# Where loads, PSUM banks and projection fill stand around the attention start of a hybrid decoder layer

## The chip, the cores and the metric

The kernel runs on one core of a Trainium2 chip. A core has five engines with queues of their own: PE (TensorE, matrix products), DVE (VectorE), ACT (ScalarE), POOL (GpSimd) and SP (SyncE, which here only issues DMAs). Transfers run on 16 DMA engines that all queues share. The metric is the device time of one execution in microseconds; lower is better.

## The reference

One layer of a decoder trunk on 1024 tokens of width 1024, with 16 learned meta tokens put in front. Everything is float32.

```python
u = rmsnorm(h, attn_norm_w[l])
proj = u @ w_in[l]
gq, gk, gv, gz, gb, ga, fq, fk, fv, ff = jnp.split(proj, IN_SPLITS, axis=-1)
o_gdn = gated_deltanet_group(jnp.concatenate([gq, gk, gv], axis=-1), gz, gb, ga, ...)
o_fox = forgetting_attention_group(fq, fk, fv, ff, fgate_b[l])
h = h + jnp.concatenate([o_gdn, o_fox], axis=-1) @ w_out[l]
h = h + swiglu(rmsnorm(h, ffn_norm_w[l]), w_gate[l], w_up[l], w_down[l])
h = rmsnorm(h, final_norm_w)
```

The first group (gated DeltaNet, 4 heads of 128) runs a delta rule over 64-token chunks: a triangular solve inside each chunk and a state carried from chunk to chunk. The second ("fox", 8 heads of 64) is causal softmax attention whose logits carry the difference of two cumulative log forget gates.

## The kernel before

Each float32 operand is split into a high part (a cast, on ACT, line 163) and a low part (the rest, on DVE, line 164); each product is three matmuls (`mm3g`, line 212): high by high, high by low, low by high. So weights that arrive by DMA (`load_w`, line 180, tiles raw_*) need two casts (whi_*, wlo_*) before PE can use them.

The program runs in stages: norms; DeltaNet projections and their convolution; the solve of the 64-token chunks, prepared by small 32-by-32 inverses (DVE steps on the tile up, lines 527 and 529); then the stage that the change touches; then attention; then the output projection of the fox half and the feed-forward network.

**Order of PE.** From the touched stage on, PE's order is written by a planner (`PeOrder`). It keeps a model time, chains with due times (generators that yield when their next step is ready), and one generator of fill. A chain step that is due runs first; otherwise the fill goes on by one matmul. The chains are `levels(0)` and `levels(1)` (the rest of the triangular solve, two heads each, due at model times that come from `LV0`), `scan()` (8 chunks of the state; po, os, on and then the transposes ot belong to it) and `csum` (the cumulative forget gate). The fill `fox()` is the projection work: z0 in 8 tiles, fv1 and fv0 (values, two column halves, one meta tile and 8 token tiles each), fk0 to fk3 and fq0 to fq3 (keys and queries, three column thirds each, named by their first column: 16, 358 and 700 for queries). What of the fill is left when the last chunk is out is run down before attention. In attention (`attention`, `scores`, `values`) the chain makes scores (sc), exponentials (pr, ACT line 1019), transposes (pt, line 1055) that ACT and DVE split into ph and pl (phm for the meta tokens), and value products (po, lines 1075, 1078 and 1079). Its fill is `wout_gdn`, the output projection of the DeltaNet half (tiles wog); DVE adds the input rows to it in ht (line 1175).

**Order of the rest.** On ACT, DVE, POOL and in SP's DMA queue the order is set by a scheduler that simulates a timeline of its own; `tc.issue_after(x)` makes it place an instruction behind x. Each queue runs in order. SP's DMAs share eight completion semaphores in turn, so each waits for the DMA eight places before it.

**Buffers.** A value tile of fv is split into fvt (3 buffers) and stored to v_d in DRAM (line 940). A key or query third is split into fhl (2 buffers, ACT line 768, DVE line 769) and stored to k_d or q_d (line 771). `att_head(h)` loads a head's keys, queries and values back (ka, qa, kk, sa, avt; lines 737 to 746) and, from head 1 on, the meta-token values: `vm_load` issues 8 loads of 8 KB per head (line 728), for heads 0 and 1 together behind head 1's loads. PSUM has one bank for general products (`ps_mm`, tag mm), two for po (tag pv, `ps_v`), two for scores, three for transposes. While `rot` is not zero, `ps_mm` turns over mm and both pv banks; at zero it gives the one mm bank.

Of the kernel before, what the change touches and what calls it, by code (L numbers as in the profile page):

```python
# [9 lines left out]
F32 = mybir.dt.float32  # L10
F32R = mybir.dt.float32r
# [4 lines left out]
P = 128  # L16
# [13 lines left out]
GQ, GK, GV, GZ, FQ, FK, FV = 0, 512, 1024, 1536, 2056, 2568, 3080  # L30
TCH = ((0, 348), (348, 346), (694, 346))
GRP = 4
LV0 = (76.0, 119.0)
LAT = 0.4
ATT0 = 3.0
LEAD = 0.6
# [61 lines left out]
def tile_hymba_layer(ctx, tc, x, meta, attn_norm_w, w_in, conv_w, a_log, dt_bias, gdn_norm_w,  # L98
                     fgate_b, w_out, ffn_norm_w, w_gate, w_up, w_down, final_norm_w, out):
    nc = tc.nc  # L100
# [11 lines left out]
    rot = [1]  # L112
# [11 lines left out]
    def ps_v(name):  # L124
        return bank("pv", 2, name)
# [469 lines left out]
    def levels(hp):  # L595
        na = lp.tile([P, 2, NT, P], F32, tag="na", bufs=2, name=f"na_{hp}")
        tb = lp.tile([P, 2, NT, 32], F32, tag="tb", bufs=2, name=f"tb_{hp}")
        ubk = lp.tile([P, 2, NT, 32], F32, tag="ubk", bufs=2, name=f"ubk_{hp}")
        nc.sync.dma_start(ubk, ud_d[hp].rearrange("b j h t k -> (b j) h t k"))
        for i in range(2):  # L600
            nc.sync.dma_start(na[:, i], rec_d[:, :, 0, 2 * hp + i].rearrange("t p c -> p t c"))
        if not hp:
            lv_t["act"], lv_t["dve"] = tail[0]
        with tc.issue_after(lv_t["dve"].ins):
# [96 lines left out]
        yield from mm3g(acc[:rows, :n], [(uh[:, k, col:col + rows], ul[:, k, col:col + rows], w[0][k][:, :n],  # L701
                                          w[1][k][:, :n]) for k in range(KT)], n / 2400)

    last = [None]

    fox_ws = [(GZ, 256, "z0"), (FV + 256, 264, "fv1"), (FV, 256, "fv0"), (FK, 256, "fk0"), (FK + 256, 256, "fk1"),
              (FQ, 256, "fq0"), (FQ + 256, 256, "fq1")]
# [1 line left out]

    def fox_load():  # L710
        if fox_ws:
            fox_w.append(win_block(*fox_ws.pop(0)))

    t_ld, hds, fixed, fq_m, h_ld = [], {}, [], [0], {}

# [203 lines left out]
    def fox():  # L919
        fox_load()  # L920
        w = fox_w.pop(0)
        for t in range(NT):
            if t == 1:
                fox_load()
            acc = ps_mm(f"z0_{t}")
            yield from proj_tmg(acc, t, w, 256)
            gate_out(t, acc, *((fvp, "fvt") if t < NT - 2 else (fp, "fhl")), 0)
        for b in (1, 0):
            n = 256 + 8 * b
            w = fox_w.pop(0)  # L930
            for t in range(-1, NT):
                if t == 1:
                    fox_load()
                col, rows = tok_cols(t)
                acc = (ps_mm if b or t % 2 else ps_t)(f"fv{b}_{t}")
                yield from proj_tmg(acc, t, w, n)
                vt = fvp.tile([P, 4, 2, DH], F32R, tag="fvt", name=f"fvt{b}_{t}")
                av = acc[:rows, :256].rearrange("p (h d) -> p h d", d=DH)
                split(vt[:rows, :, 0], vt[:rows, :, 1], av)
                nc.sync.dma_start(v_d[4 * b:4 * b + 4, col:col + rows].rearrange("h t d -> t h d"),  # L940
                                  vt[:rows].rearrange("p h a d -> p h (a d)").bitcast(F32))
                if b:
                    nc.vector.tensor_copy(fr[:rows, NT if t < 0 else t], acc[:rows, 256:264])
        fvc.close()
        yield from fox_proj(lambda m: k_d[m], TCH, 0, 1.0, "fk")
        od.add(csum(), od.t + 8.0)
        yield from fox_proj(lambda m: q_d[m].rearrange("a p c -> p a c"), ((NM, 342), (NM + 342, 342), (NM + 684, 340)), NM, -DH ** -0.5, "fq")

    lv_left, outs_left = {0, 1}, set(range(NT))
    for hp in range(2):  # L950
        od.add(levels(hp), LV0[hp] - 8.0)
    od.fill = fox()
    peo = ExitStack()
    peo.enter_context(tc.manual_schedule(engines={mybir.EngineType.PE}))
# [12 lines left out]
    od.add(scan(), od.t + 4.0, front=True)  # L967
    od.run(lambda: not outs_left)
    scc.close()
    while od.step_fill():  # L970
        pass
    uctx.close()

    alc = ExitStack()
    als.append(alc.enter_context(tc.tile_pool(name="alo", bufs=1)))
    atc = ExitStack()
    ap_ = atc.enter_context(tc.tile_pool(name="ap", bufs=1, side="right"))
    ap2 = atc.enter_context(tc.tile_pool(name="ap2", bufs=1, side="right"))
    rsum = ap_.tile([P, FH, NT], F32, name="rsum")
    for i in range(2):  # L980
        vms.append(ap2.tile([P, GRP, P], F32R, name=f"vm{i}"))
        nc.gpsimd.memset(vms[i].bitcast(F32), 0.0)
    att_tiles(1)
    masks = []

    def scores(h, g, hd, out):
# [54 lines left out]
    def values(h, g, hd, pts):  # L1041
# [1 line left out]
        nk = GRP * (g + 1)  # L1043
        nm = f"{g}_{h}"
        box = []
        for kt in (0, -1, *range(1, nk)):
            c0, j0 = NM + P * kt, max(0, kt - GRP * g)
            yield max(r for _, r in pts)
            pt = ps_t(f"pt_{nm}_{kt}")
# [18 lines left out]

            def av(kt=kt, ph=ph, pl=pl, q=q):
                if kt == 0:  # L1070
                    box.append(ps_v(f"po_{nm}"))
                po = box[0]
                if kt < 0:
                    for j in range(GRP):
                        nc.tensor.matmul(po[:, P * j:P * j + P], vms[h % 2][:, j], ph, start=False, stop=False)
                    od.pe(0.2135)
                    return
                nc.tensor.matmul(po[:, q], vt[:, kt], ph[:, q], start=kt == 0, stop=False)
                nc.tensor.matmul(po[:, q], vt[:, kt], pl[:, q], start=False, stop=(kt == nk - 1))
                od.pe((512 - q.start) / 1200)  # L1080
                if kt == nk - 1:
                    oa = ap2.tile([P, 512], F32, tag="oa", bufs=2, name=f"oa_{nm}")
                    nc.scalar.copy(oa, po)
                    od.on("act", 0.5)
                    for i in range(2):
                        last_o[0] = nc.gpsimd.dma_start(
                            o_d[GRP * g:GRP * g + GRP, rows, 4 * i + m].rearrange("t p c -> p t c"),
                            v3(oa[DH * i:DH * i + DH], GRP))
# [4 lines left out]
    def attention():  # L1093
# [3 lines left out]
        def score_stream():  # L1097
            for i, (h, g) in enumerate(groups):
                if h not in hds:
                    with tc.issue_after(last[0].ins) if h == 1 else nullcontext():  # L1100
                        hds[h] = att_head(h)
                ptl[i] = []
                for n, rdy in enumerate(scores(h, g, hds[h], ptl[i])):
                    pos[0] = i + n / (5, 9)[g]
# [10 lines left out]
                yield r  # L1115

        yield from ahead(1.0)
        rot[0] = 0
        for i, (h, g) in enumerate(groups):
            nt = GRP * (g + 1) + 1  # L1120
            yield from ahead(i + 1.0)
# [607 lines left out]
```

## Time and profile before

| what | value |
|---|---|
| median of three runs | 1305.55 us (1304.69 to 1306.87) |
| the profiled execution | 1305.29 us |
| its span, first to last instruction | 1303.6 us, mean granted TensorE clock 0.996 |
| PE busy | 1281.6 us, 98% of the span |
| DVE, ACT, POOL busy | 839.7, 547.7, 348.8 us |
| moved by DMA | 232.07 MB, mean 178 GB/s |

PE is the engine to watch: idle PE time is what a change of order can win or lose. The projection and scan stage lies between about 200 and 440 us, attention between 440 and 590, and the rest is the output projection and the feed-forward network. In rows of a timeline the bracket at the end gives the engine's idle time before the instruction, and what it waited for.

### The profile page before, as it was taken

Reading aid. Unit: us, or ns where it says so; the run is one execution under the profiler, and the core shown is the slowest. Engines: PE = TensorE matmul, PEld = TensorE weight load, DVE = VectorE, ACT = ScalarE, POOL = GpSimd, SP = SyncE. Lnnn points to the kernel's source line nnn. Section 1 sums busy time; section 2 is a strip of 40 time slices with the busy share of each in tenths; the row PEclk is TensorE's granted clock in tenths of the full one; section 3 lists DMA queues with packets and bytes.
Section 4 is the critical chain, followed back from the end, with each engine's and each line's share of the span. In section 5 each row is a group of like instructions: output and inputs, shape, how many; then the busy total and the mean of one; then the engine's idle time right before and its main releaser. Section 6 shows DMA issues by size and latency. Waiting matters only on the chain.

```text
span 1303.6 us, 20023 instructions
## 1 busy us (share of the span) xinstructions
PE 1281.6 (98%) x7434; PEld 1127.5 (86%) x7434; DVE 839.7 (64%) x1508; ACT 547.7 (42%) x940; POOL 348.8 (27%) x316
## 2 busy tenths in 40 slices
PE   9999999899999999999999999999999999999997
PEld 8999999899999888887778888888888888888886
DVE  6667898583246768886887666556666664365645
ACT  6455444142223557884553333233333343433332
POOL 2012213101022221112504534455334443020301
PEclk9999999999999999999999999999999999999999
DMA  6333625854389886737435644553444467945513
GB/s 230 99 118 110 183 86 141 234 143 154 127 285 304 220 236 190 183 94 253 168 114 161 198 165 155 186 163 129 159 155 166 165 212 268 393 178 197 207 64 129
DMA packets 185248, 232.07 MB, mean 178 GB/s; under 512 B 19816, under 2 KB 138176, under 8 KB 182336
## 3 DMA queue, kind: packets, MB, share of 16 engines
q1 hardware_dynamic: 182256, 222.15, 53.1%
q0 software_dynamic: 2896, 8.65, 2.2%
q8 instruction: 58, 0.95, 0.3%
q14 instruction: 38, 0.31, 0.1%
HBM read 153.11 MB, written 77.65 MB: 177 GB/s over the span
## 4 chain that ended last, share of the span: by engine, by line
PE 87%; DVE 5%; DMA 3%; issue 2%; SPq 1%; ACT 1%; POOL 0%; POOLq 0%; DVEq 0%; ACTq 0%
PE xp L1610 9%; PE yp L1610 7%; PE ua L1435 5%; PE ga L1435 5%; PE gb L1435 5%; PE ud L1435 5%; PE gd L1435 5%; PE ub L1435 5%; PE pj_fk L212 4%; PE pj_fq L212 3%; PE fv L212 3%; PE ue L1435 2%; PE ge L1435 2%; PE pt L1055 2%; PE wog L212 2%
## 5 line engine op out<-in xcount | busy, mean ns | idle before, releaser
L164 DVE TENSOR_TENSOR al_p<-ra_p,ah_p 128x2048 fp32r<-128x2048 f32 (+1 forms) x21 | 47.7, 2273 | 94.5 <-ACT ah_p L163 94.5
L163 ACT CAST ah_p<-ra_p 128x2048 fp32r<-128x2048 f32 (+1 forms) x21 | 37.1, 1767 | 106.2 <-PE xp L1610 47.9
L1610 PE MATMUL xp<-wl_p,ah_p 128*128 128x512 f32 (+1 forms) x176 | 67.3, 382 | 0.0
L1610 PE MATMUL xp<-wh_p,al_p 128*128 128x512 f32 (+1 forms) x176 | 67.3, 382 | 0.0
L1610 PE MATMUL xp<-wh_p,ah_p 128*128 128x512 f32 (+1 forms) x176 | 67.3, 382 | 0.0
L1491 POOL TENSOR_TENSOR gzw<-gzw,uzt 128x512 f32<-128x512 f32 x11 | 18.4, 1673 | 168.0 <-DVE uzt L1480 138.9
L1435 PE MATMUL gb<-uh_p,w_g_p 128*128 128x512 f32 x176 | 57.8, 389 | 0.0
L1435 PE MATMUL ub<-uh_p,w_u_p 128*128 128x512 f32 x176 | 57.7, 389 | 0.0
L1435 PE MATMUL gd<-uh_p,w_g_p 128*128 128x512 f32 x176 | 57.7, 389 | 0.0
L1435 PE MATMUL ud<-uh_p,w_u_p 128*128 128x512 f32 x176 | 57.7, 389 | 0.0
L163 ACT CAST ph<-pt 128x512 fp32r<-128x512 f32 (+1 forms) x96 | 45.2, 474 | 29.8 <-PE pt L1055 28.8
L164 DVE TENSOR_TENSOR pl<-pt,ph 128x512 fp32r<-128x512 f32 (+1 forms) x96 | 52.0, 554 | 8.4 <-ACT ph L163 7.8
L1491 POOL TENSOR_TENSOR gxy<-gxy,uxy 128x512 f32<-128x512 f32 x22 | 39.0, 1771 | 64.7 <-DVE uxy L1480 53.7
L164 DVE TENSOR_TENSOR w_u_p<-raw_u,w_u_p 128x512 fp32r<-128x512 f32 x42 | 41.9, 997 | 21.6 <-ACT w_u_p L163 21.5
L1019 ACT ACTIVATE pr<-pr,sm 128x144 f32<-128x144 f32 (+3 forms) x64 | 50.5, 791 | 10.0 <-DVE sm L1014 9.8
L1435 PE MATMUL ua<-uh_p,w_u_p 128*128 128x512 f32 x160 | 52.5, 389 | 0.0
L1435 PE MATMUL ga<-uh_p,w_g_p 128*128 128x512 f32 x160 | 52.5, 389 | 0.0
L1610 PE MATMUL yp<-wh_p,ah_p 128*128 128x512 f32 x132 | 51.3, 389 | 0.0
L1610 PE MATMUL yp<-wl_p,ah_p 128*128 128x512 f32 x132 | 51.3, 389 | 0.0
L1610 PE MATMUL yp<-wh_p,al_p 128*128 128x512 f32 x132 | 51.3, 389 | 0.0
L163 ACT CAST w_u_p<-raw_u 128x512 fp32r<-128x512 f32 x42 | 26.0, 620 | 55.7 <-PE gd L1435 36.0
L164 DVE TENSOR_TENSOR wl_p<-rw_p,wh_p 128x2048 fp32r<-128x2048 f32 (+1 forms) x21 | 46.5, 2212 | 3.8 <-ACT wh_p L163 3.8
(649 smaller groups left out, 4233.0 us busy)
## 6 DMA issues: line engine op xcount, KB each, us to landing
ra_p<-ao_p SPq DMA_DIRECT2D x14, 1024.0 KB
raw_g<-in_w_gate_dram SPq DMA_DIRECT2D x22, 512.0 KB
raw_u<-in_w_up_dram SPq DMA_DIRECT2D x22, 512.0 KB
raw_d<-in_w_down_dram SPq DMA_DIRECT2D x22, 512.0 KB
wt_p<-raw_d SPq DMA_DIRECT2D x33, 256.0 KB
rw_p<-wt_p SPq DMA_DIRECT2D x8, 1024.0 KB
rw_p<-in_w_down_dram SPq DMA_DIRECT2D x6, 1024.0 KB
ao_p<-gzw SPq DMA_DIRECT2D x22, 256.0 KB
```

The costliest lines, as they stand in the source:

```text
L163: cast = nc.scalar.copy(dst_hi, src)
L164: low = nc.vector.tensor_sub(dst_lo, src, dst_hi.bitcast(F32))
L212: nc.tensor.matmul(dst, a, b, start=first, stop=last)
L1019: nc.scalar.activation(pr[:, :n], pr[:, :n], AF.Exp, bias=sm[:, np_ - 1:np_], scale=-1.0, accum_out=rsum[:, h, j:j + 1])
L1055: nc.tensor.transpose(pt[:, P * j:P * j + P], pts[j][0][:, j, c0:c0 + P], ident)
L1435: nc.tensor.matmul(dst, a[:, c], b[:, k], start=(first and k == 0 and i == 0), stop=(k == 3 and i == 2), skip_group_check=not first)
L1491: last_mul[0] = G.tensor_tensor(gs[d], gs[d], us[d], op=ALU.mult)
L1610: nc.tensor.matmul(dst[:, n_], a[:, f, c], b[:, f, n_], start=(first and i == 0 and n == 0), stop=(i == NF - 1 and n == 2), skip_group_che ...
```

## The change

- `LV0` is smaller, and the levels' chains are added 20 instead of 8 below it: the solve, and with it the scan, enter PE's order sooner.
- The loads of the levels (ubk, na) are placed behind the last key or query store, or, where there is none yet, behind the last value store (`vst`). The projection weights' loads, while no key or query store exists, are placed behind the last value store.
- The tiles of attention that head 1 uses, the memsets of vm and head 1's loads are requested right after the scan's last chunk, ahead of the fill that is left; the clause that put head 1's loads behind the last query store is gone. As two heads' loads have then been requested when attention's fill starts, the loads of ht that SP issued go to POOL.
- In `values`, for the second half of the queries of a head (8 key tiles), the meta tile comes after the fourth key tile instead of after the first.
- `rot` becomes zero with the first po and not before the first value step, so attention's fill turns over three banks until then.

```diff
--- before.py
+++ after.py
@@ -30,7 +30,7 @@
 GQ, GK, GV, GZ, FQ, FK, FV = 0, 512, 1024, 1536, 2056, 2568, 3080
 TCH = ((0, 348), (348, 346), (694, 346))
 GRP = 4
-LV0 = (76.0, 119.0)
+LV0 = (72.0, 106.0)
 LAT = 0.4
 ATT0 = 3.0
 LEAD = 0.6
@@ -596,9 +596,10 @@
         na = lp.tile([P, 2, NT, P], F32, tag="na", bufs=2, name=f"na_{hp}")
         tb = lp.tile([P, 2, NT, 32], F32, tag="tb", bufs=2, name=f"tb_{hp}")
         ubk = lp.tile([P, 2, NT, 32], F32, tag="ubk", bufs=2, name=f"ubk_{hp}")
-        nc.sync.dma_start(ubk, ud_d[hp].rearrange("b j h t k -> (b j) h t k"))
-        for i in range(2):
-            nc.sync.dma_start(na[:, i], rec_d[:, :, 0, 2 * hp + i].rearrange("t p c -> p t c"))
+        with tc.issue_after((last[0] or vst[0]).ins):
+            nc.sync.dma_start(ubk, ud_d[hp].rearrange("b j h t k -> (b j) h t k"))
+            for i in range(2):
+                nc.sync.dma_start(na[:, i], rec_d[:, :, 0, 2 * hp + i].rearrange("t p c -> p t c"))
         if not hp:
             lv_t["act"], lv_t["dve"] = tail[0]
         with tc.issue_after(lv_t["dve"].ins):
@@ -701,7 +702,7 @@
         yield from mm3g(acc[:rows, :n], [(uh[:, k, col:col + rows], ul[:, k, col:col + rows], w[0][k][:, :n],
                                           w[1][k][:, :n]) for k in range(KT)], n / 2400)
 
-    last = [None]
+    last, vst = [None], [None]
 
     fox_ws = [(GZ, 256, "z0"), (FV + 256, 264, "fv1"), (FV, 256, "fv0"), (FK, 256, "fk0"), (FK + 256, 256, "fk1"),
               (FQ, 256, "fq0"), (FQ + 256, 256, "fq1")]
@@ -709,7 +710,8 @@
 
     def fox_load():
         if fox_ws:
-            fox_w.append(win_block(*fox_ws.pop(0)))
+            with tc.issue_after(vst[0].ins) if vst[0] and not last[0] else nullcontext():
+                fox_w.append(win_block(*fox_ws.pop(0)))
 
     t_ld, hds, fixed, fq_m, h_ld = [], {}, [], [0], {}
 
@@ -937,7 +939,7 @@
                 vt = fvp.tile([P, 4, 2, DH], F32R, tag="fvt", name=f"fvt{b}_{t}")
                 av = acc[:rows, :256].rearrange("p (h d) -> p h d", d=DH)
                 split(vt[:rows, :, 0], vt[:rows, :, 1], av)
-                nc.sync.dma_start(v_d[4 * b:4 * b + 4, col:col + rows].rearrange("h t d -> t h d"),
+                vst[0] = nc.sync.dma_start(v_d[4 * b:4 * b + 4, col:col + rows].rearrange("h t d -> t h d"),
                                   vt[:rows].rearrange("p h a d -> p h (a d)").bitcast(F32))
                 if b:
                     nc.vector.tensor_copy(fr[:rows, NT if t < 0 else t], acc[:rows, 256:264])
@@ -948,7 +950,7 @@
 
     lv_left, outs_left = {0, 1}, set(range(NT))
     for hp in range(2):
-        od.add(levels(hp), LV0[hp] - 8.0)
+        od.add(levels(hp), LV0[hp] - 20.0)
     od.fill = fox()
     peo = ExitStack()
     peo.enter_context(tc.manual_schedule(engines={mybir.EngineType.PE}))
@@ -967,20 +969,21 @@
     od.add(scan(), od.t + 4.0, front=True)
     od.run(lambda: not outs_left)
     scc.close()
+    alc = ExitStack()
+    als.append(alc.enter_context(tc.tile_pool(name="alo", bufs=1)))
+    for i in range(2):
+        vms.append(als[1].tile([P, GRP, P], F32R, name=f"vm{i}"))
+        nc.gpsimd.memset(vms[i].bitcast(F32), 0.0)
+    att_tiles(1)
+    hds[1] = att_head(1)
     while od.step_fill():
         pass
     uctx.close()
 
-    alc = ExitStack()
-    als.append(alc.enter_context(tc.tile_pool(name="alo", bufs=1)))
     atc = ExitStack()
     ap_ = atc.enter_context(tc.tile_pool(name="ap", bufs=1, side="right"))
     ap2 = atc.enter_context(tc.tile_pool(name="ap2", bufs=1, side="right"))
     rsum = ap_.tile([P, FH, NT], F32, name="rsum")
-    for i in range(2):
-        vms.append(ap2.tile([P, GRP, P], F32R, name=f"vm{i}"))
-        nc.gpsimd.memset(vms[i].bitcast(F32), 0.0)
-    att_tiles(1)
     masks = []
 
     def scores(h, g, hd, out):
@@ -1043,7 +1046,7 @@
         nk = GRP * (g + 1)
         nm = f"{g}_{h}"
         box = []
-        for kt in (0, -1, *range(1, nk)):
+        for kt in (0, -1, 1, 2, 3) if nk == GRP else (0, 1, 2, 3, -1, *range(4, nk)):
             c0, j0 = NM + P * kt, max(0, kt - GRP * g)
             yield max(r for _, r in pts)
             pt = ps_t(f"pt_{nm}_{kt}")
@@ -1068,6 +1071,7 @@
 
             def av(kt=kt, ph=ph, pl=pl, q=q):
                 if kt == 0:
+                    rot[0] = 0
                     box.append(ps_v(f"po_{nm}"))
                 po = box[0]
                 if kt < 0:
@@ -1097,8 +1101,7 @@
         def score_stream():
             for i, (h, g) in enumerate(groups):
                 if h not in hds:
-                    with tc.issue_after(last[0].ins) if h == 1 else nullcontext():
-                        hds[h] = att_head(h)
+                    hds[h] = att_head(h)
                 ptl[i] = []
                 for n, rdy in enumerate(scores(h, g, hds[h], ptl[i])):
                     pos[0] = i + n / (5, 9)[g]
@@ -1115,7 +1118,6 @@
                 yield r
 
         yield from ahead(1.0)
-        rot[0] = 0
         for i, (h, g) in enumerate(groups):
             nt = GRP * (g + 1) + 1
             yield from ahead(i + 1.0)
```

How the order moves. SP around the first value stores (v_d<-fvt1_t: value tile t, column half 1; raw_fv0: weights of the other half; raw_fk0: key weights; na and ubk: inputs of the levels), before:

```order
L599 DMA ubk_0_3280<-ud_d_101 128x512
L307 DMA rec_d_99<-zt0_7_2713 128x256
L601 DMA na_0_3278<-rec_d_99 128x8x128
L180 DMA raw_fk0_0_3056<-in_w_in_dram 128x4x256
L601 DMA na_0_3278<-rec_d_99 128x8x128
L601 DMA na_1_3762<-rec_d_99 128x8x128
L180 DMA raw_fk0_1_3062<-in_w_in_dram 128x4x256
L601 DMA na_1_3762<-rec_d_99 128x8x128
L940 DMA v_d_106<-fvt1_-1_2741 16x4x128
```

and now:

```order
L307 DMA rec_d_99<-zt0_7_2713 128x256
L942 DMA v_d_106<-fvt1_-1_2741 16x4x128
L942 DMA v_d_106<-fvt1_0_2771 128x4x128
L180 DMA raw_fv0_0_2776<-in_w_in_dram 128x4x256
L180 DMA raw_fv0_1_2782<-in_w_in_dram 128x4x256
L942 DMA v_d_106<-fvt1_1_2813 128x4x128
L942 DMA v_d_106<-fvt1_2_2843 128x4x128
```

The first two value stores moved ahead of the loads of ubk, na and raw_fk; the two loads of raw_fv0, which stood far ahead, come behind the second store.

ACT at the same place, as the difference of the two orders (whi_fv0: weight casts; fvt1_t: value casts):

```order
-L163 CAST whi_fv0_0_2778<-raw_fv0_0_2776 128x1024
 L306 ACTIVATE zt0_7_2713<-z0_7_2688 128x256
-L163 CAST whi_fv0_1_2784<-raw_fv0_1_2782 128x1024
 L163 CAST fvt1_-1_2741<-fv1_-1_2716 16x4x64
 L163 CAST fvt1_0_2771<-fv1_0_2746 128x4x64
 L163 CAST fvt1_1_2813<-fv1_1_2788 128x4x64
+L163 CAST whi_fv0_0_2778<-raw_fv0_0_2776 128x1024
 L163 CAST fvt1_2_2843<-fv1_2_2818 128x4x64
+L163 CAST whi_fv0_1_2784<-raw_fv0_1_2782 128x1024
```

The two weight casts moved behind the third and the fourth value cast.

PE at the end of the scan (ot_6 and ot_7 are the last chunks' transposes; pj_fq: query projection; wog: output projection; sc: scores), before:

```order
L212 MATMUL pj_fq3_700_4887<-uh_118,whi_fq1_0_3888 128x340
...
L874 MATMUL ot_6_4912<-ident_63,on_6_4843 128x128 x4
L212 MATMUL pj_fq3_700_4887<-uh_118,wlo_fq1_0_3889 128x340
...
L874 MATMUL ot_7_4936<-ident_63,on_7_4901 128x128 x4
L212 MATMUL wog_0_0_4983<-whi_wo0_00_4971,uh_p5_4091 128x512
...
L1009 MATMUL sc_0_0_0_0_5005<-ka0_4104,qa0_4105 128x144
```

and now:

```order
L212 MATMUL pj_fq2_358_4760<-uh_118,wlo_fq1_1_4030 128x342
...
L876 MATMUL ot_6_4801<-ident_63,on_6_4732 128x128 x4
L212 MATMUL pj_fq2_358_4760<-ul_119,whi_fq1_1_4029 128x342
...
L212 MATMUL pj_fq2_700_4820<-uh_118,whi_fq1_0_4023 128x340
...
L876 MATMUL ot_7_4845<-ident_63,on_7_4790 128x128 x4
L212 MATMUL pj_fq3_16_4897<-uh_118,whi_fq1_0_4023 128x342
...
L212 MATMUL pj_fq3_358_4926<-uh_118,whi_fq1_0_4023 128x342
...
L212 MATMUL pj_fq3_700_4955<-uh_118,whi_fq1_0_4023 128x340
...
L212 MATMUL wog_0_0_5011<-whi_wo0_00_4999,uh_p5_3935 128x512
...
L1012 MATMUL sc_0_0_0_0_5033<-ka0_3948,qa0_3949 128x144
```

Between ot_6 and ot_7 stood 13 matmuls of the last query third and none after ot_7; now 32 of block 2 stand between them and 72 of block 3 after them. Over the whole scan, 87 projection matmuls moved from ahead of its first product to behind it.

SP at the start of attention (kk_1 to avt_1: head 1's loads; vm0 and vm1: the meta values; q_d<-fhl: query stores), before:

```order
L771 DMA q_d_104<-fhl_fq3_700_4932 128x2x340
L737 DMA ka1_4961<-c_d_107 3x1040
L738 DMA qa1_4962<-c_d_107 3x1024
L741 DMA kk_1_5128<-k_d_105 64x1040
L742 DMA sa_1_5129<-q_d_104 64x1024
L741 DMA kk_1_5128<-k_d_105 64x1040
L742 DMA sa_1_5129<-q_d_104 64x1024
L743 DMA ka1_4961<-k_d_105 64x1040
L744 DMA qa1_4962<-q_d_104 64x1024
L746 DMA avt_1_5138<-v_d_106 128x8x128
L728 DMA vm0_4957<-v_d_106 16x128 x8
L728 DMA vm1_4959<-v_d_106 16x128 x8
```

and now:

```order
L773 DMA q_d_104<-fhl_fq2_358_4816 128x2x342
L744 DMA sa_1_4866<-q_d_104 64x1024
L743 DMA kk_1_4865<-k_d_105 64x1040
L739 DMA ka1_4861<-c_d_107 3x1040
L740 DMA qa1_4862<-c_d_107 3x1024
L744 DMA sa_1_4866<-q_d_104 64x1024
L745 DMA ka1_4861<-k_d_105 64x1040
L746 DMA qa1_4862<-q_d_104 64x1024
L748 DMA avt_1_4875<-v_d_106 128x8x128
L730 DMA vm0_4857<-v_d_106 16x128 x8
L730 DMA vm1_4859<-v_d_106 16x128 x8
L773 DMA q_d_104<-fhl_fq2_700_4893 128x2x340
```

The last query store stood ahead of head 1's loads. Now the store of the last third of query block 2 stands behind head 1's loads and all sixteen vm loads, and three more query stores follow it. The ACT cast of fhl_fq3_358, which waits for that store's buffer, stands ahead of the first exponential.

## The prediction

> **What bounds the kernel now.** I read the page's engine shares and the clock per core first, then the table of windows, then what PE (TensorE) waited for, then the places of those waits row by row.
>
> ```profile
> PE 1281.6 (98%) x7434; PEld 1127.5 (86%) x7434; DVE 839.7 (64%) x1508; ACT 547.7 (42%) x940; POOL 348.8 (27%) x316
> core 0: 1303.6 us, clock 0.996
> 440.00:460.00 20.00, 17.83 (x86) 13.84 (x85) 12.60 (x39) 8.69 (x22) 5.52 (x10) 1.00 0.90 234
> 680.00:880.00 200.00, 200.00 (x884) 165.59 (x883) 128.74 (x182) 61.73 (x104) 92.94 (x59) 1.00 0.52 170
> ```
>
> Columns of the windows: length, then busy time and count of PE, its weight loads, DVE, ACT, POOL, then the granted clock, the DMA share and GB/s. PE bounds the kernel. From 680 us on it never idles, and the change does not touch that part, so only idle PE time between about 190 and 600 us can be won. No matmul is removed. What PE waited for between 190 and 680 us:
>
> ```profile
> PE fv L212 <- DVE fr L943: 3.3, 1, 3.3
> PE wog L212 <- DVE ht L1175: 2.4, 3, 0.8
> PE po L1079 <- DVE pl L164: 1.4, 5, 0.3
> PE ot L874 <- DVE on L868: 1.0, 1, 1.0
> PE po L1075 <- DVE phm L164: 0.9, 1, 0.9
> ```
>
> (Total, times, longest.) These five rows are 9.0 us; each is touched by the edit. That is the most the edit can win, apart from clock and restart losses behind the waits. The edit also moves DMA issues in SP's queue, which these rows cannot show.
>
> **The value-store wait.** Four views of it: PE, ACT, SP's queue, the chain, then windows.
>
> ```profile
> 253.79 0.56 PE L212 MATMUL fv<-whi_fv,uh 128*128 128x264 f32 x1 [3.27 <-DVE fr L943]
> 252.74 0.37 ACT L163 CAST fvt<-fv 128x256 fp32r<-128x256 f32 x1 [10.57 <-DMA v_d<-fvt_-1_2741]
> 240.67 0.41 DVE L164 TENSOR_TENSOR fvt_-1_2741<-fv_-1_2716,fvt_-1_2741 16x256 fp32r<-16x256 f32 x1
> 243.42 2.19 SPq L180 DMA_DIRECT2D raw_fk<-in_w_in_dram  x1
> 246.58 1.61 SPq L940 DMA_DIRECT2D v_d<-fvt_-1_2741  x1
> 246.58 6.07 DMA v_d<-fvt_-1_2741
> 254.00:256.00 2.00, 2.00 (x10) 2.00 (x11) 1.90 (x7) 0.37 (x1) 0.00 (x0) 0.50 0.48 146
> 256.00:258.00 2.00, 2.00 (x16) 2.00 (x16) 1.90 (x7) 0.00 (x0) 0.00 (x0) 0.82 0.40 124
> 258.00:260.00 2.00, 2.00 (x19) 2.00 (x18) 1.90 (x7) 0.37 (x1) 0.00 (x0) 1.00 0.43 131
> ```
>
> The first value tile was split by 241.08, but its store was issued at 246.58, behind a load of raw_fk among others, and landed 6.07 us later. There are three fvt buffers, so ACT's fourth cast waited for that store, the PSUM bank of that tile stayed full, and PE stopped for 3.27 us. Behind the stop the clock fell to 0.50: 10 and then 16 matmuls ran in 2 us where 19 run at full clock, 12 matmuls short at 2.00/19 = 0.105 us, so 1.3 us more. The wait costs 3.27 + 1.3 = 4.6 us.
>
> The change puts ubk, na and raw_fk behind stores, so the store goes at about 242 and lands before the cast needs its buffer. But the loads of raw_fv, in before long past, go behind the second value store, and ACT's order now has the weight cast whi_fv ahead of the fourth fvt cast. Late next is therefore that weight.
>
> ```profile
> 242.94 0.42 DVE L164 TENSOR_TENSOR fvt<-fv,fvt 128x256 fp32r<-128x256 f32 x1
> L163 ACT CAST whi_fv<-raw_fv x4: 1038/1064/1076, 195.0 to 233.3; 128x1056 fp32r<-128x1056 f32 x2, 128x1024 fp32r<-128x1024 f32 x2
> L164 DVE TENSOR_TENSOR wlo_fv<-raw_fv,whi_fv x4: 1226/1238/1257, 196.3 to 234.4; 128x1056 fp32r<-128x1056 f32 x2, 128x1024 fp32r<-128x1024 f32 x2
> 615.38 3.25 DMA hst<-h_d
> 234.28 5.60 DMA ad<-ad_d
> 250.24 0.28 PE L212 MATMUL fv<-whi_fv,ul 128*128 128x264 f32 x1
> ```
>
> The second tile is split at 243.36; store and load issue take SP to about 244.6. The nearest load of 512 KB (hst) landed in 3.25 us, so 247.9; the slowest nearby one (ad) took 5.60, so 250.2. Then whi_fv 1.05, and on DVE wlo_fv 1.24, a step of the inverse 0.3, the fvt split 0.4 and fr 0.2: the bank is free at 251.1 to 253.4, against PE ready just after 250.24 and 0.12 us per matmul. The residue is 0.8 to 3.1 us; I take 1.2, nearer to hst because na and raw_fk have left this stretch. Clock loss after it: none, since the 1.0 us wait at ot (below) left 1.00. Term: 1.2 - 4.6 = **-3.4** (bounds -4.6 and -1.5; with the clock loss at the slow end, -0.2).
>
> **End of the scan.** The planner now starts the levels and the scan earlier, so 87 projection matmuls that came before the scan's first product come after it: more fill remains behind the last chunk. The wait at ot goes, because 32 projection matmuls stand between the last two ot steps instead of 13: **-1.0**. What hides it is projection work of 32 x 0.156 us.
>
> ```profile
> 433.01 2.03 PE pj_fq L212 x13
> 437.95 0.36 DVE on L868
> 438.45 1.06 PE L874 MATMUL ot<-ident,on 128*128 128x128 f32 x4 [0.95 <-DVE on L868]
> 438.00:440.00 2.00, 1.55 (x7) 1.15 (x8) 2.00 (x6) 1.51 (x4) 1.67 (x3) 1.00 0.29 102
> ```
>
> An earlier scan may meet inputs or DVE work not ready. No row of PE shows such a wait at the old times; I put 0 to 2, taken as **+0.7**.
>
> **Attention's fill.** The first output-projection tiles (wog) used one PSUM bank; now three turn over until the first po.
>
> ```profile
> 455.14 0.53 PE L212 MATMUL wog<-whi_wo,uh_p 128*128 128x512 f32 x1 [0.79 <-DVE ht L1175]
> L1175 DVE TENSOR_TENSOR ht<-wog,ht x10: 681/691/693, 442.3 to 592.4; 128x512 f32<-128x512 f32 x10
> ```
>
> Three waits of 0.79, each with a first matmul of 0.53 instead of the median 0.39: 3 x 0.93 = **-2.8**. In return the second po group finds its bank held by the third wog until ht (0.69 plus the step) is done: **+0.9**, bounds 0 and 0.9.
>
> In the second group of each head, the meta-token tile now stands between tiles 3 and 4, so four leading tiles pass before it. The five pl waits (1.4, plus about 0.1 at each restart) go: **-2.0**, bounds -1 and -2.3. The phm wait (0.9) becomes smaller, since fill is spread to head 5 instead of 3: **-0.6**, bounds -0.9 and +0.5.
>
> **The new wait.** Head 1's loads and its 16 vm loads are now requested ahead of the remaining fill, without the clause that put them behind the last projection store. In SP's order the query store of block 2, last third, stands behind eight loads of head 1 and sixteen vm loads. The fhl tag has two buffers, so the ACT split two thirds later waits for it, holding the bank that the second wog tile needs; queued behind on ACT are the first exponentials and on DVE the first score sums.
>
> ```profile
> 440.90 0.38 SPq L771 DMA_DIRECT2D q_d<-fhl_fq  x1
> 441.37 0.29 SPq L737 DMA_DIRECT2D ka<-c_d  x1
> 445.88 0.50 SPq L744 DMA_DIRECT2D qa<-q_d  x1
> 446.43 0.70 SPq L746 DMA_DIRECT2D avt<-v_d  x1
> 447.23 14.49 SPq L728 DMA_DIRECT2D vm<-v_d  x16
> L728 SPq DMA_DIRECT2D vm<-v_d x64: 302/318/2907, 447.2 to 561.4; - x64
> SPq L744 <- DMA q_d<-fhl_fq: 0.5, 1, 0.5
> SPq L728 <- DMA avt<-v_d: 1.2, 1, 1.2
> ```
>
> Count in the clock of before, held at the scan's end. Head 1's buffers come free with the last on step (438.3). Its loads took 5.1 us to issue (441.37 to 446.43), so the vm loads start near 444. If nothing holds them they go at 0.318 plus 0.05 each: 16 x 0.37 = 5.9, to 450. In before they took 14.49, because each waits for the DMA eight places earlier, head 1's own large loads (the avt row is one of five of this kind): that is 458.5. The store issued at 440.90 was still awaited just before 445.88, 4.9 us; the lightest store here, of oa, took 2.67 (quoted below). Then 1.0 for the split. The bank is free between 450 + 2.7 + 1.0 = 453.7 and 458.5 + 4.9 + 1.0 = 464.4.
>
> ```profile
> 591.42 2.67 DMA o_d<-oa
> 439.51 2.79 PE wog L212 x12
> ```
>
> PE gets there thus: the 13 pj_fq matmuls end at 435.0, ot 0.5, then 32 x 0.156 = 5.0, ot 0.5, 72 x 0.156 = 11.2, wog 2.8 and two score pairs, 455.4. The stall lies between 0 and 9.0 us. The nearest row is before's own vm loop with the same loads ahead, but three ht loads have left SP's queue; I take two thirds, 6.0, plus the 1.3 us of clock that a stop over 3 us cost above: **+7.3**. Nothing hides it: PE runs in order.
>
> The Trainium skill ("DMA: Bandwidth & Descriptors", Anatomy of one DMA) fits a lone transfer at 2.0 us plus bytes over 436 GB/s. By it a 260 KB head load takes an estimated 2.6 us and the vm loads would never be held; the trace does not agree for this stretch (the vm loop took 14.49 us). That rule would give the first rival.
>
> Sum: -3.4 - 1.0 + 0.7 - 2.8 + 0.9 - 2.0 - 0.6 + 7.3 = -0.9 us. The profiled run took 1305.29 (span 1303.6 plus 1.7), 0.26 under the median of 1305.55. Forecast 1305.29 - 0.9 = **1304.4**: gains and the new stall nearly cancel.
>
> **Rivals.** (1) SP drains at issue speed, no stall at the second wog tile. For: issue itself is short (318 ns). Against: SP's waits for the head's own loads. The sum without 7.3 is -8.2: **1297.1**. (2) Slower: the SP queue holds the store longer than in before. Now POOL issues five ht loads and the weight loads and two more stores join the same stretch; DMA share was 0.90 already in 440 to 460. At 12 us of stall plus 1.3, the sum is -8.2 + 13.3 = +5.1: **1310.4**. It decides from a stall of 9.8 us on (-8.2 + 11.1 = +2.9, past the 0.2% named below). Against: before's loop, with more on SP, bounds it at 9.0. (3) The value wait does not shrink, because the weight load takes over: -0.2 instead of -3.4, **1307.6**. For: ACT runs in order and the load now starts at 244. Against: the first load would have to take 5.6 us. (4) The change does not do what it says: the planner's fill count could leave the old waits at ot, wog and pl standing, with a stall of 3 us: -3.4 + 0.7 - 0.6 + 3.0 = -0.3, **1305.0**. For: one column of due times moves many chains at once. Against: the order already shows the fill behind the last chunk.
>
> Clock page: the Trainium skill ("TensorE: Matmul & The Clock Gate", HAM oscillation) puts the idle gap that halves the clock at more than about 3.4 us. The trace shows 0.50 after a wait of 3.27, so the point here is no higher than that, and by the page a stall of 6 us is well inside: an estimated 1.7 us lost at half rate, where the row gives 1.3.
>
> **How the numbers follow.** This kernel's times separate from no change at about 0.2%, 2.6 us: faster means under 1302.9, slower over 1308.2. Chances: forecast 0.40, rival 1 0.28, rival 2 0.17, rival 3 0.10, rival 4 0.05. The forecast's own range, stall 3 to 9 us, is 1300 to 1307.4. Faster: all of rival 1 and 0.08 of the forecast's low end, 0.36. Slower: rival 2 and 0.06 of rival 3, 0.23. Same: 0.41. The range reaches down to rival 1 less 0.6 and up to 1309.5, leaving out about half of rival 2 and little below.
>
> **What would show it.** Right: PE's wait at fv falls to about 1 us with a clock of 1.00 behind it, and ACT's wait before whi_fv names the raw_fv load; the rows wog from ht, po from pl and ot from on vanish; SP shows sixteen vm loads and then the query store; ACT shows a wait of several us before fhl_fq from that store, PE a wait of 3 to 9 us at wog (or at the scores beside it), and a window of clock under 1.00 after it. Wrong: no wait there (rival 1), or more than 9.8 us (rival 2), or fv still at 3 us (rival 3), or new waits in the scan above 2 us. A chain of waits that leads through levels before the scan would show that starting it early costs what the sum left at 0.7.

## The result

| | median | lowest to highest |
|---|---|---|
| kernel before | 1305.92 us | 1304.69 to 1306.87, 4 runs |
| changed kernel | 1313.65 us | 1312.18 to 1316.10, 4 runs |
| ratio | 1.0058 | 95% interval 1.0044 to 1.0072 |

The change is slower by 0.6%, 7.7 us at the medians. The forecast was 1304.4, a gain of 0.9 us, in a range up to 1309.5; the measured time lies above that range. The profiled executions took 1305.29 and 1312.18, 6.9 us apart, and their traces tell where.

PE's first matmuls of three stages cut both programs at points with the same work behind them: the key projection (all value tiles done), the DeltaNet output projection (projections and scan done), and the fox output projection (attention done). In the four stretches that these points cut, PE ran 2004, 1364, 921 and 3150 matmuls before, and 2003, 1364, 922 and 3150 now (a record can be missing). PE's timeline before:

```profile
289.35 0.32 PE L212 MATMUL pj_fk<-uh,whi_fk 128*128 128x348 f32 x1
439.26 0.48 PE L212 MATMUL wog<-whi_wo,uh_p 128*128 128x512 f32 x1
595.48 0.46 PE L202 MATMUL wof<-whi_wo,ohl 128*128 128x512 f32 x1
```

and of the changed kernel:

```profile
286.12 0.32 PE L212 MATMUL pj_fk<-uh,whi_fk 128*128 128x348 f32 x1
442.22 0.39 PE L212 MATMUL wog<-whi_wo,uh_p 128*128 128x512 f32 x1
602.92 0.39 PE L202 MATMUL wof<-whi_wo,ohl 128*128 128x512 f32 x1
```

| stretch | before | changed | difference | forecast |
|---|---|---|---|---|
| to the key projection | 289.35 | 286.12 | -3.2 | -3.4 |
| key projection to end of scan | 149.91 | 156.10 | +6.2 | -0.3 |
| attention | 156.22 | 160.70 | +4.5 | +2.8 |
| rest, to the execution's end | 709.81 | 709.26 | -0.6 | 0 |

So the value store did what was worked out, attention lost somewhat more than forecast, and the middle stretch, where almost nothing was expected, lost 6 us.

### The profile page after: what moved, and what is told of

It reads as the page before. It is cut to its first block, busy times and chain, and to the rows that moved or that the text cites. A ratio compares the mean times of both kernels' runs of the same rounds, so it can differ in the third digit from the quotient of the medians.

```text
span 1310.4 us, 19999 instructions
## 1 busy us (share of the span) xinstructions
PE 1280.5 (98%) x7434; PEld 1128.9 (86%) x7434; DVE 837.8 (64%) x1508; ACT 546.6 (42%) x940; POOL 352.2 (27%) x319
## 4 chain that ended last, share of the span: by engine, by line
PE 77%; DMA 8%; DVE 8%; issue 3%; SPq 2%; ACT 2%; POOL 0%; POOLq 0%; DVEq 0%; ACTq 0%
PE xp L1612 9%; PE yp L1612 7%; PE ua L1437 5%; PE ga L1437 5%; PE gb L1437 5%; PE ud L1437 5%; PE gd L1437 5%; PE ub L1437 5%; PE pj_fk L212 3%; PE pt L1058 2%; PE ue L1437 2%; PE ge L1437 2%; PE wog L212 2%; PE sc L1012 1%; PE po L1083 1%
```

## The profile after

PE's waits from 190 us to the end of attention in the changed kernel (total, times, longest; one of 0.2 left out):

```profile
PE wog L212 <- DVE fhl_fq L771: 8.8, 1, 8.8
PE py L648 <- DVE u L638: 3.5, 2, 3.1
PE sc L1012 <- DVE sm L1017: 1.7, 3, 0.6
PE po L1083 <- DVE pl L164: 1.1, 2, 0.5
PE fv L212 <- DVE fr L945: 1.0, 1, 1.0
PE pvn L833 <- DVE r L828: 0.8, 1, 0.8
PE fv L212 <- DVE up L529: 0.4, 1, 0.4
```

The waits at ot, at wog from ht and at phm are gone, and fv fell from 3.3 to 1.0 and 0.4. Two new ones stand above them. The first, at py in the levels, is one that the prediction did not name. DVE and PE at that place:

```profile
292.74 0.41 DVE L527 TENSOR_TENSOR amt<-amt 4x256 f32<-4x256 f32 x1
299.95 0.21 DVE L787 TENSOR_TENSOR ubm<-umt,beta 16x64 f32<-16x64 f32 x1 [5.94 <-DMA umt<-um_d]
300.10 1.39 DVE L638 COPY u<-pu 32x512 f32<-32x512 f32 x2
300.82 0.41 PE L648 MATMUL py<-ident,u 64*64 64x64 f32 x4 [3.15 <-DVE u L638]
```

and pieces of the chain of waits that leads there:

```profile
284.23 5.91 DMA v_d<-fvt
...
290.24 0.37 ACT fvt L163
290.62 0.96 ACT whi_fk L163
291.60 1.22 DVE wlo_fk L164
...
293.67 2.96 DMA um_d<-amt
...
296.69 3.24 DMA umt<-um_d
```

A value store that landed 5.91 us after its issue held ACT's next value cast; behind that cast stood the weight cast whi_fk, behind it DVE's wlo_fk, and behind that the last steps of the mask solve (amt, a small inverse on DVE). Its result goes to DRAM as um_d and comes back as umt; DVE multiplies it into ubm. The scan needs ubm only for a product at 359 us. But in DVE's order ubm stands ahead of the copy into u that PE needs at once, and DVE stood still in front of it for 5.94 us. Before, ubm stood ahead of that copy too, and it did no harm: the solve was done sooner, ubm ran without a wait, and the copy came 13 us later:

```profile
285.45 0.41 DVE L527 TENSOR_TENSOR amt<-amt 4x256 f32<-4x256 f32 x1
290.37 0.21 DVE L785 TENSOR_TENSOR ubm<-umt,beta 16x64 f32<-16x64 f32 x1
303.29 1.40 DVE L637 COPY u<-pu 32x512 f32<-32x512 f32 x2 [5.10 <-PE pu L633]
```

The stop cost more than its 3.5 us, as the windows around it show (PE, weight loads, DVE, ACT, POOL, then the granted clock):

```profile
300.00:302.00 2.00, 0.77 (x8) 0.59 (x8) 1.94 (x4) 0.00 (x0) 0.00 (x0) 0.93 0.00 0
302.00:304.00 2.00, 2.00 (x18) 1.77 (x16) 0.04 (x1) 0.58 (x1) 0.00 (x0) 0.50 0.37 138
304.00:306.00 2.00, 2.00 (x8) 1.99 (x8) 0.00 (x0) 0.58 (x1) 0.00 (x0) 0.50 0.11 39
306.00:308.00 2.00, 2.00 (x13) 1.62 (x11) 0.00 (x0) 0.00 (x0) 0.00 (x0) 0.50 0.00 0
308.00:310.00 2.00, 2.00 (x39) 1.76 (x38) 0.83 (x2) 0.86 (x2) 0.40 (x1) 0.87 0.03 8
```

Half clock for three windows and parts of the two beside them: 2 x (0.07 + 0.5 + 0.5 + 0.5 + 0.13) = 3.4 us. With 3.5 of waiting that is 6.9 for the new stop; the 1.0 us at ot went and 0.8 came at pvn.

The second is the stall that was forecast. PE, ACT, SP's queue, the store (issue and time to landing), and windows:

```profile
454.43 0.80 PE L212 MATMUL wog<-whi_wo,uh_p 128*128 128x512 f32 x1 [8.82 <-DVE fhl_fq L771]
453.37 0.46 ACT L770 ACTIVATE fhl_fq<-pj_fq 128x342 fp32r<-128x342 f32 x1 [9.77 <-DMA q_d<-fhl_fq]
435.60 14.82 SPq L730 DMA_DIRECT2D vm<-v_d  x16
450.52 2.77 DMA q_d<-fhl_fq
454.00:456.00 2.00, 1.57 (x4) 1.39 (x5) 0.89 (x2) 1.18 (x5) 0.00 (x0) 0.50 0.99 277
456.00:458.00 2.00, 2.00 (x7) 1.72 (x7) 0.94 (x4) 0.72 (x2) 0.00 (x0) 0.50 1.04 389
458.00:460.00 2.00, 2.00 (x11) 1.77 (x10) 0.92 (x4) 0.55 (x1) 0.00 (x0) 0.82 0.47 167
```

The vm loop took 14.82 us, like before's 14.49 and unlike the 5.9 estimated for a loop that nothing holds; the store behind it was issued at 450.52. Half clock followed from 454.43, where PE began again, to about 458.7 (0.82 in the last window is half clock for 0.7 us): half of these 4.3 us, 2.1 us, was lost. Wait and half clock are 10.9 us, while the stretch of attention lost 4.5. Waits of 2.4 at wog from ht, 0.9 at phm and 0.3 at pl are gone, and the waits at sc grew by 1.0; some 4 us of gain stand in no wait and stay open.

## Experiments

Differences between versions are worked out from their ratios to the kernel before, run beside them, times 1306 us.

**1. One DVE instruction moved.** In the changed kernel:

```diff
-        V.tensor_mul(ub, umt, beta[:NM, NT, :, None].broadcast_to([NM, GH, NM]))
+        with tc.issue_after(lv_t["dve"].ins):
+            V.tensor_mul(ub, umt, beta[:NM, NT, :, None].broadcast_to([NM, GH, NM]))
```

> The changed kernel with one DVE instruction moved: the product ubm (umt times beta), which the scan needs only 60 us later, is placed behind the last copy into u of the levels instead of ahead of it. Theory (queue): the 3.1 us wait of PE at py and the half clock behind it come from DVE standing 5.9 us in front of ubm for the round trip of um through DRAM, with the copy PE needs queued behind it. Then PE's waits at py vanish, the clock stays 1.00 between 298 and 310 us, and the time falls by 5 to 6.5 us, to about 1307.5. Rival (due times): the levels are simply asked for before their inputs are there; then another wait takes the place of this one and the time stays at 1312 to 1314.

Measured: 1307.60 us (1306.18 to 1309.99), ratio to before 1.0013 (1.0004 to 1.0022). Against the changed kernel's 1.0058 that is 5.9 us less. No wait at py is left; the copy into u waits only for its own product, and the clock stays full:

```profile
295.66 1.40 DVE L638 COPY u<-pu 32x512 f32<-32x512 f32 x2 [1.63 <-PE pu L634]
300.00:304.00 4.00, 4.00 (x56) 3.63 (x55) 0.84 (x2) 1.06 (x2) 1.12 (x2) 1.00 0.02 4
```

The wait at wog stands (9.7 against 8.8). The levels' inputs were there at the earlier due times. What PE waited for was the place of a bystander in DVE's queue.

**2. The vm loads alone behind the last query store.** `att_head(1)` no longer calls `vm_load`; behind the fill stands

```diff
     while od.step_fill():
         pass
+    with tc.issue_after(last[0].ins):
+        vm_load(0)
+        vm_load(1)
     uctx.close()
```

> The changed kernel with the sixteen vm loads of heads 0 and 1 placed behind the last query store; head 1's other loads stay where the change put them. Theory (SP queue): the 8.8 us wait at the second wog tile is the query store standing behind the vm loads; it falls under 1 us, and with the clock loss behind it the time falls by 9 to 10 us, to about 1304. Rival (meta values late): the vm loads are then late for the first po product, PE waits there for most of what it gained, and the time stays above 1308.

Measured: 1310.09 us, ratio 1.0033 (1.0021 to 1.0045): 3.3 us gained, not 9 to 10. Neither story fits as it was written. No wait at po for the meta values came, so the rival's reason is out. But PE still waited 3.3 us at wog, and 2.0 at a score step:

```profile
PE wog L212 <- DVE fhl_fq L770: 3.3, 1, 3.3
PE sc L1014 <- DVE sm L1019: 2.6, 2, 2.0
```

ACT shows the wait behind it, and the chain the store that it waited for:

```profile
447.03 0.46 ACT L769 ACTIVATE fhl_fq<-pj_fq 128x342 fp32r<-128x342 f32 x1 [6.13 <-DMA q_d<-fhl_fq]
434.68 12.27 DMA q_d<-fhl_fq
436.00:440.00 4.00, 4.00 (x28) 4.00 (x27) 0.00 (x0) 0.45 (x1) 0.00 (x0) 1.00 1.04 248
```

No vm load stood ahead of the store any more, and SP came to it at 434.68, as soon as it was split. But from there to its landing took 12.27 us (3.35 of them SP's issue, where the median is 0.40), against 2.77 in the changed kernel, where head 1's loads had landed by then. All DMA engines were busy in this time, with head 1's other loads and five loads of ht (share 1.04 in the window). What is left is the traffic of early loads, more than their place in SP's queue.

**3. Both edits.**

> Both edits of the two runs before together in the changed kernel. If the two waits are separate, the gains add: 1313.6 - 6 - 9.5 = about 1298, which is 0.6% under the kernel before. If the second only shifts into other waits of attention, 1302 to 1306.

Measured: 1303.76 us, ratio 0.9985 (0.9976 to 0.9993), inside the range of the second expectation. From run 1 to this one 3.7 us, from run 2 to this one 6.3; alone the two edits gave 3.3 and 5.9. The gains add. The sum missed 1298 because the edit of the vm loads is worth under 4, not 9.5.

**4. Head 1's loads back behind the last query store**, with ubm moved (`hds[1] = att_head(1)` taken out ahead of the fill):

```diff
-                    hds[h] = att_head(h)
+                    with tc.issue_after(last[0].ins) if h == 1 else nullcontext():
+                        hds[h] = att_head(h)
```

> The changed kernel with ubm moved as before and with all of head 1's loads put back behind the last query store, at attention's first score step; every other part of the change stays. Theory (SP queue): the waits at the second wog tile (9.7 us with ubm moved, 3.6 with only the vm loads moved) are entirely head 1's loads and vm loads ahead of the query stores, so none is left and nothing else gets late: 1303.8 - 3.6 - 1.6 and a little = 1298 to 1301. Rival (loads late): head 1's loads come so late now that the first scores of head 1 or the first po wait: 1303 or more.

Measured: 1298.27 us (1298.13 to 1302.55), ratio to before 0.9951 (0.9938 to 0.9963). It beats both kernels: 0.5% (6.4 us) under the one before, 1.1% (14.0 us) under the changed one. The wait at wog is gone, and head 1's loads, issued from 439.49 on, were not missed:

```profile
PE po L1083 <- DVE pl L164: 2.1, 4, 0.5
PE sc L1012 <- DVE sm L1017: 1.1, 2, 0.6
```

From run 1 to this one it is 8.1 us by the ratios (9.3 between the medians): that is what requesting head 1 early cost the changed kernel. It is less than the wait (9.7) and the half clock behind it together: run 4 waits 1.1 us more for pl, and the rest of this is not explained. Without ubm's place (5.9) and this (8.1) the rest of the change gains 6.4.

**5. Query stores of blocks 2 and 3 issued by POOL**, head 1 still early on SP, ubm moved:

```diff
-                    last[0] = nc.sync.dma_start(dst(m)[:, :, c0 - off:c0 - off + n], hl[:, :, :n].bitcast(F32))
+                    last[0] = (nc.gpsimd if off and m > 1 else nc.sync).dma_start(dst(m)[:, :, c0 - off:c0 - off + n], hl[:, :, :n].bitcast(F32))
```

> The changed kernel with ubm moved as before and with the query stores of blocks 2 and 3 issued by POOL instead of SP; head 1's loads stay early on SP. Theory (order in SP's queue): the stores no longer stand behind the vm loads, the wait at wog goes, 1307.6 - 9 = 1298 to 1300. Rival (the DMA engines themselves): the stores share the engines with the same loads and land late all the same; the wait at wog stays at 4 us or more, 1302 to 1306.

Measured: 1301.69 us, ratio 0.9968 (0.9957 to 0.9979): between run 1 and run 4. The wait at wog falls from 9.7 to 3.2. The chain that leads to what is left starts at a store that POOL issued at 426.87 and that landed 11.56 us later, while the DMA engines were busy throughout:

```profile
426.87 11.56 DMA q_d<-fhl_fq
438.53 0.46 ACT L770 ACTIVATE fhl_fq<-pj_fq 128x342 fp32r<-128x342 f32 x1 [11.85 <-DMA q_d<-fhl_fq]
432.00:436.00 4.00, 4.00 (x28) 4.00 (x27) 0.00 (x0) 0.00 (x0) 0.00 (x0) 1.00 1.02 246
```

So the place in SP's queue is the larger part of the wait, and the rest has the rival's form: a store that lands late beside the same loads. How much of the 11.56 us comes from POOL's own queue, where three ht loads stood ahead of this store, the trace does not separate. (POOL issued the store after it only at 436.69, after 7.96 us of idle time for which the trace names nothing; that is not the store that PE's wait hung on.)

**6. Value-store part alone, in the kernel before** (only the `vst` places of the diff, with a guard for loads that come before any store).

> The kernel before with one part of the change alone: the loads of ubk and na and the projection weights' loads are placed behind value stores; due times, attention and head 1 are as before. Theory: the wait at fv falls from 3.3 to about 1 us with no half clock behind it, and nothing else moves: 1305.9 - 3.0 = 1302.9. Rival (late weights): the weights of keys and the mask solve behind them on DVE become late, and the levels wait for them even at the old due times: 1305 to 1309.

Measured: 1305.11 us, ratio 0.9991 (0.9982 to 1.0). The fv wait falls to 1.1 as expected, but a small new wait stands beside it:

```profile
PE fv L212 <- DVE fr L945: 1.1, 1, 1.1
PE py L623 <- DMA na<-rec_d: 0.8, 1, 0.8
```

The levels wait for na, now loaded behind stores. The key projection starts at 286.31, 3.0 us earlier than before; the output projection starts 2.1 us earlier in this profile than in before's, and the timed runs show 1.2.

**7. Earlier due times alone, in the kernel before.**

> The kernel before with the earlier due times of the levels alone. Theory (queue): here the loads stay where they were, the mask solve is done early, ubm has its data when DVE comes to it, and PE waits nowhere at py; the ot wait of 1.0 goes and a first scan wait of about 1.3 comes: 1305 to 1306.5. Rival (due times): the levels are asked for before their inputs are there even so, and it costs several us: 1308 to 1312.

Measured: 1305.92 us, ratio 1.0001 (0.9992 to 1.0009): as the first theory had it. The ot wait goes, a wait of 1.1 at pvn comes, and ubm costs next to nothing:

```profile
291.49 0.21 DVE L785 TENSOR_TENSOR ubm<-umt,beta 16x64 f32<-16x64 f32 x1 [0.69 <-DMA umt<-um_d]
```

**8. Both of these together.**

> The kernel before with two parts of the change together, the loads behind value stores and the earlier due times; attention and head 1 are as before. Alone they measured 1305.1 and 1305.9 against 1305.8 and 1306.2. Theory (the two together): the loads behind stores make the mask solve on DVE late, and the early levels come to its product ubm before its data; only together do they make the wait at py, so it stands here at about 3 us with the half clock behind it: 1305.1 + 6.0 = 1309 to 1312. Rival (sum of parts): no new wait, 1304 to 1306, and the wait of the changed kernel needs something of the attention part.

Measured: 1307.80 us, ratio 1.0013 (1.0004 to 1.0022). By the ratios of runs 6 and 7 the parts sum to -1.1 us; together they are +1.7. The wait at py is there, with DVE standing in front of ubm:

```profile
298.50 0.21 DVE L787 TENSOR_TENSOR ubm<-umt,beta 16x64 f32<-16x64 f32 x1 [5.08 <-DMA umt<-um_d]
PE py L648 <- DVE u L638: 2.5, 2, 2.1
```

In run 6 DVE stood in front of ubm too, for 2.57 us, but there the copy came only at 301.23. So the stop belongs to the combination: loads behind stores delay the mask solve, and the early due times bring the copy that queues behind its product. The total is under the 1309 I had as the lower end, since this stop is shorter by 1 us.

**9. The two attention edits alone, in the kernel before.**

> The kernel before with the two attention edits alone: the meta tile in mid-group and the three banks until the first po; due times and all loads as before. My prediction's terms for these (-2.8 wog, +0.9 second po, -2.0 pl, -0.6 phm) give -4.5: 1301.4. Rival, from the changed kernel's trace, where two waits at pl of 0.5 and score waits of 0.6 stand in place of the five of 0.3: the lead edit moves waits rather than removing them, and the sum is -2 to -3: 1303 to 1304.

Measured: 1303.78 us, ratio 0.9981 (0.9971 to 0.9991). That is -2.5 us: the rival's figure, not the prediction's -4.5. Four pl waits of 0.5 stand where five of 0.3 stood:

```profile
PE po L1080 <- DVE pl L164: 2.1, 4, 0.5
PE sc L1009 <- DVE sm L1014: 1.1, 2, 0.6
```

The wait at phm (0.9) is gone, but the waits for pl and sc grew from 1.4 and 0.7 to 2.1 and 1.1: the three together were 3.0 us before and are 3.2 here.

**10. Three banks until the first po alone** (the two `rot` lines).

> The kernel before with three banks until the first po alone. The prediction gave it -2.8 for the three waits at wog and +0.9 for the second po: 1304.2. By the trace with both attention edits, where no wait at the second po stands, it is -2.9: 1303.2.

Measured: 1303.13 us, ratio 0.9973 (0.9964 to 0.9983), 3.5 us under before. The three waits at wog are gone and none at the second po came; within the intervals the whole gain of run 9 is here. (This profile's own execution took 1306.70, at the upper end of its runs, with a wait of 4.2 at fv, so the verdict rests on the timed runs.)

**11. The meta tile back behind the first key tile**, in the version of run 4:

```diff
-        for kt in (0, -1, 1, 2, 3) if nk == GRP else (0, 1, 2, 3, -1, *range(4, nk)):
+        for kt in (0, -1, *range(1, nk)):
```

> The version with ubm moved and head 1 put back, with the meta tile back behind the first key tile in the second group. The prediction gave the mid-group place -2.0 for the pl waits and -0.6 for phm: by that this run takes about 1300.9. By the traces since (four pl waits of 0.5 stand where five of 0.3 stood, and score waits of 0.6 came) the place moves waits and is worth 0 to 1 us: 1298 to 1299.5.

Measured: 1299.68 us, ratio to before 0.9948 (0.9935 to 0.9960), against 0.9951 in run 4. By the ratios the two are the same: the mid-group place is worth nothing that can be measured.

**12. Loads behind stores and the attention edits, without the earlier due times.**

> The kernel before with the loads behind value stores and the two attention edits, without the earlier due times and with head 1 as before: the version with ubm moved and head 1 put back (1298.3), less the earlier due times. If the due times are worth nothing when ubm is out of the way, as they were alone, this one takes 1298 to 1300; if they give the rest, the sum of the two measured parts holds: -0.7 - 2.5 = 1302 to 1303.5.

Measured: 1301.00 us (1299.51 to 1302.78), ratio 0.9959 (0.9946 to 0.9971). It lies between the two expectations. The intervals of this run and of run 4 overlap, so whether the earlier due times help at all once ubm is out of the way stays open; one cost they avoid is na, for which this profile shows PE waiting 1.2 us at py.

## Why the prediction was wrong

**Value store: right, the residue in part by luck.** The term was -3.4, the stretch up to the key projection moved by -3.2, with a residue of 1.0 to 1.4 us at fv where 1.2 was taken and a clock of 1.00 behind it. The late item is the one that was named:

```profile
248.84 1.05 ACT L163 CAST whi_fv<-raw_fv 128x1024 fp32r<-128x1024 f32 x1 [6.95 <-DMA raw_fv<-in_w_in_dram]
```

But the row for the load was misread: the hst load at 615.38 (3.25 us) is one of 256 KB, not of 512 KB. The first raw_fv load, issued at 244.38, took about 4.4 us; PE stopped 0.4 us later as well (at 250.93, before at 250.52), so the residue stayed small. Alone the part is worth less (-1.2 in run 6, with an interval of 1.2 to each side). In its profile the 3.0 us are there at the key projection and 1.0 is lost again by the output projection, 0.8 of it at na. That this load moves too was in the text, but its reader was not followed.

**"An earlier scan may meet inputs or DVE work not ready ... 0 to 2, taken as +0.7": this is the step that failed.** It measured +5.9 (run 1). No row of before could show such a wait, and from that a small figure was made instead of following DVE's order as ACT's had been followed for the value casts: ubm stands ahead of the copy into u in it. The bound of 2 had no row behind it. Two things were missed together. The mask solve shares DVE with the weight casts that the change made late; its last step moved from 285.45 to 292.74. And a stop of over 3 us brings 3.4 us of half clock with it, a cost that the prediction knew and applied to the other stall only. Runs 6 to 8 show that neither part alone makes the stop, so a sum of parts could not have found it.

**End of the scan, -1.0: right in place, given back.** The ot wait went; 0.8 came at pvn. By run 7 the earlier due times alone are worth nothing.

**The new wait at wog, +7.3: right in mechanism, too small.** 6.0 us of wait were taken out of 0 to 9.0; the wait was 8.8, almost the upper end, since the vm loop ran as it had in before (14.82 against 14.49 us) in spite of the ht loads that had left SP. The deduction of a third had no row for it. Half clock cost about 2.1 rather than 1.3. What its removal returns is 8.1 us (run 4). Run 2 corrects the story: the vm loads are 3.3 of it, head 1's other loads the rest. In runs 2 and 5 a store that no vm load held back in the queue took 12.27 and 11.56 us to land, where the prediction had taken 2.7 to 4.9; in run 4, without head 1's loads in this stretch, no such wait is left.

**Banks, -2.8 and +0.9:** the first is about right (-3.5 in run 10, with an interval of 1.3 to each side). The second did not appear.

**Meta tile, -2.0, and phm, -0.6: wrong.** The wait at phm goes, the waits for pl move from one tile to another and get longer: nothing measurable (runs 9 and 11).

**The rivals.** Rival 2 (a stall over 9.8 us) gave 1310.4 and the right sign, but not by its mechanism: the stall stayed at 8.8, under the point from which it was to decide. Rival 1 is out: the vm loop was held as in before. In the changed kernel SP waited in it for the head's own loads:

```profile
SPq L730 <- DMA ka<-k_d: 2.0, 1, 2.0
SPq L730 <- DMA qa<-q_d: 1.7, 1, 1.7
```

The Trainium skill ("DMA: Bandwidth & Descriptors", Anatomy of one DMA) gives the 2.0 us plus bytes over 436 GB/s for DMAs that GpSimd issues, and these loads are SP's. The trace does not agree for them in this stretch: head 1's avt load took 11.68 us to land.

What stays open: the parts measured alone in the kernel before (-1.2, +0.1, -2.5 in runs 6, 7 and 9) sum to -3.6, while the version that holds them all without the two stalls has -6.4. Waits of 0.8 at na and 0.9 at ot, which stand in run 6's profile and not in run 4's, may be 1.7 of the difference; the rest is within what the intervals leave open. None of this was tested.

## What to carry to other kernels

When an edit makes an engine's work earlier or later, read the whole order of every in-order engine between the new place and the old one, and ask for each instruction in it what it waits for; a bystander that waits for a round trip through DRAM stops all that is queued behind it. Early loads are not free where stores share their queue or the DMA engines: what matters is who waits for the store behind them. And price a stall of a few microseconds with the clock that is lost after it.

## What the runs showed of the hardware

The half clock behind a stop lasted for very different times. After 3.27 us of idle in the kernel before, full clock was back about 2.9 us after the first matmul (0.82 in the window from 256 on); after 8.82 us in the changed kernel, about 4.3 us after it; after 3.15 us at py it took 7.7 us, from 300.82 to about 308.5. There PE ran transposes and 64-by-64 products, with gaps, before the wide matmuls and again behind them. The Trainium skill ("TensorE: Matmul & The Clock Gate", Part 1: The HAM clock gate) gives about 3.4 us of sustained work for the return to full clock; the first two cases agree roughly, the third took more than twice as long. The same page (Part 4: PE-mode transpose) says that transposes do not count as PE work in the same way, which would fit, but no run here separates the transposes from the gaps.

The clock did not fall at the same point of a stop either. In the kernel before it fell at about 253.3, 2.8 us after PE had stopped (0.83 in the window from 252 to 254). At py it fell at about 301.7 (0.93 in the window from 300 on), 4.0 us after PE had stopped and 0.9 us after it had begun again with transposes. Idle times of 3.15 and 3.27 us were followed by half clock, one of 0.95 us, at ot in the kernel before, was not.
